# One hybrid decoder layer: p as a unit of the weight stream, six swap tiles, attention pieces at later slots

## The chip, the core and the metric

The kernel runs on one core of a Trainium2 chip. The metric is the device time of one execution in microseconds (us). TensorE (PE) multiplies, VectorE (DVE) and ScalarE (ACT) do elementwise work, GpSimd (POOL) does a little, and SyncE (SP) and ScalarE issue the DMAs.

## The reference

One decoder layer on 512 tokens of width 2048, in float32:

```
h = rms_norm(x); z = h @ w_in      # attn q,k,v (8 heads) and ret q,k,v,gate (8 heads) of 128
a = attention(rotated rms_norm(q), rotated rms_norm(k), v)     # two blocks of 256: causal over all
r = silu(gate) * rms_norm(retention(rotated q, rotated k, v))
x = x + concat(a, r) @ w_o
x = x + (silu(h2 @ w_gate) * (h2 @ w_up)) @ w_down             # h2 = rms_norm(x)
x = x + (p @ w_ple_proj) * sigmoid(rms_norm(x) @ w_ple_gate + b)
```

p is 512 x 256, w_ple_proj 256 x 2048. Each product is made of three products of halves: every float32 operand is split into a high part H (ScalarE copy, written as fp32r) and a low part L = value - H (VectorE), and `mm3` adds HH, HL and LH in PSUM.

## The kernel before, in words

**First stage** (0 to 48 us): `Plain` computes q and k of head pair 0 from xT, whose 16 chunks (`h_chunk`) are loaded, scaled and split into `h` as the weights of the eight units are; step i of `run` calls `beside(i)`, which loads chunks and also forms `first_factors`, the seven combined operands for the next stage. The result goes to DRAM (`zd`).

**Second stage** (to 296 us): groups of seven-product matmuls for v and the gate, written to `vd` and `sgd`.

**Mix stage** (296 to about 795 us): for i = 1 to 7, `projection` computes q and k of head pair i (pairs 0 to 3 attention, 4 to 7 retention) from eight units of weights, each 256 x 512. A unit is four accumulators x two halves x three matmuls; `tick()` opens a slot every two accumulators, so a slot is 12 matmuls and a projection 16 slots. `weights()` keeps up to three units ahead, in the three buffers of `wq`. `heads(i)` puts the pieces of pair i into slots counted from where projection i ended, so they run on TensorE between the matmuls of projection i+1: `turn` transposes q and k (tiles z, line 667) through `tp` (two PSUM banks) into qkH and qkL; `scores` multiplies into `at` (two banks), adds the mask, and makes the softmax rows `pt` (lines 680 to 688); `weights` transposes pt (line 701) into PH and PL; `result` multiplies with v. For the retention pairs the pieces are `load`, `scores`, `normed`, `result`. TensorE keeps program order here; DVE and ACT run in an order that a list scheduler has fixed.

After a projection the four accumulators are evacuated: for attention by `evac` (L627 z, L633 to 637 the norm, L644 to 646 rotation and scaling, with m made by ACT and POOL; z0 is pair 0's input read back from `zd`); for retention by L720 (zr, an ACT copy), two DMAs that swap the halves into mr (L723, L724, issued by ACT), three DVE products and a split into qkH, qkL. z of attention and the tile bc lie in four `rp` buffers; z0, m, zr, mr, praw and pp in the `rm` buffers, four of them. The finished pair is turned into seven factor pairs by `mixed`; they are spilled to DRAM (mix<-o, L188, SP) through the four "o" tiles. `load_ropeT`, at the start of projection 4, transposes rstd (L97) and copies the bank to bc (L586).

**p projection** (759 to 795 us): p is loaded (praw), split (pT), and multiplied with four units w_pp; each accumulator is copied (pp, L858) and stored. Beside it ACT issues 13 DMAs `back` (L801), which load the spilled factors (s<-mix). The pieces of pair 7 run in its slots.

**The rest** (to 2452 us): w_o, SwiGLU, down, gate: seven-product groups, untouched by the change.

Of the kernel before, what the change touches and what calls it, by code (L numbers as in the profile page):

```python
# [11 lines left out]
F32R = mybir.dt.float32r  # L12
# [5 lines left out]
P = 128  # L18
T = 512
D = 2048  # L20
NB = T // P
NC = D // P
NS = D // 512
HD = 128
NPAIR = 4
# [8 lines left out]
def layer_kernel(ctx, tc, x, xT, pT, g_mix, wqk, w_vg, qk_norm, g_ret, w_ow, g_ffn,  # L34
                 w_gu, w_dn, g_ple, w_pl, b_pg, w_pp,
                 ident_c, rope_c, ropeT_c, decay_c, mask_c, out):
    nc = tc.nc
# [444 lines left out]
    def beside(i):  # L482

        if -2 <= i < NC // 2 - 2:
            for k in (2 * i + 4, 2 * i + 5):
                t = h_chunk(k)
                split(h[:, k, 0, :], h[:, k, 1, :], t)
            first.load(i + 2)
        if 2 <= i < 2 + NC // 2:
            first_factors(i - 2)  # L490
        for at, q in ((3, "11"), (6, "12"), (8, "22")):
            if at <= i < at + 4:
                groups[0].load(q, i - at)
        if 7 <= i < 23:
            b, s = divmod(i - 7, NS)
            t = ev_tile("o", 4, name="xn")
            nc.sync.dma_start(t, x[b * P:(b + 1) * P, s * T:(s + 1) * T])
            sq = ev_tile("o", 4, name="sq")
            nc.scalar.activation(sq, t, AF.Square, accum_out=ssq[0][:, b, s:s + 1])
        elif i == 23:  # L500
            rstd_of(ssq[0], rstd[0])
# [29 lines left out]
        return ev2.tile(list(shape), F32, name=name, tag="rp", bufs=4)  # L531

    def rm_tile(name, shape=(P, T), dt=F32):
        return ev2.tile(list(shape), dt, name=name, tag="rm", bufs=4)

    hT = [(h[:, k, 0, :], h[:, k, 1, :]) for k in range(NC)]
    tags = ["l1", "bd", "c"]

    stream = [wqk[i, u] for i in range(1, 2 * NPAIR) for u in range(NC // 2)] + [w_pp[n] for n in range(NS)]
    ready = []  # L540

    def weights():
        while stream and len(ready) < 3:
            tags.append(tags.pop(0))
            raw = rawq.tile([P, 2, T], F32, name="raw", tag=tags[0])
            wh = wq.tile([P, 2, T], F32R, name="wh", tag="wh")
            wl = wq.tile([P, 2, T], F32R, name="wl", tag="wl")
            nc.sync.dma_start(raw, stream.pop(0))
            split(wh, wl, raw)
            ready.append((wh, wl))  # L550
        return ready.pop(0)
# [107 lines left out]
    def attend(z, v, j):  # L659

        got, pts, ps = [], {}, []
# [41 lines left out]
                split(blocks(PH), blocks(PL), tp[:, :nk].rearrange("p (k c) -> p k c", c=P))  # L703

        def result():
            o = weighted(v, ps, j)
            a = ev_tile("A", name="o")
            nc.scalar.activation(a, o, AF.Copy)
            return a
# [27 lines left out]
    def retain(qk, v, j, h):  # L737
# [25 lines left out]
        def normed():  # L763
            hd = slice(j * HD, (j + 1) * HD)
            PH, PL = own["p"]
            r = own["r"] = rp_tile("r", (P, NB, HD))
            ms = stat.tile([P, NB], F32, name="ms")
            for half in range(2):
                o = at_p.tile([P, 2, 2, HD], F32, name="at", tag="at")
                for qb in (2 * half, 2 * half + 1):  # L770
                    for kb in range(qb + 1):
                        at = slice(384 * kb + qb * P, 384 * kb + (qb + 1) * P)
                        matmul(o[:, qb % 2], PH[:, at], v[:, kb, :, hd], start=kb == 0, stop=False)
                        matmul(o[:, qb % 2], PL[:, at], v[:, kb, :, hd], start=False, stop=kb == qb)
                both = slice(2 * half, 2 * half + 2)
                nc.scalar.activation(r[:, both], o[:, :, 0], AF.Copy)
                plus(r[:, both], r[:, both], o[:, :, 1])
            sq = ap.tile([P, T], F32, name="pt", tag="pt", bufs=2)
            for qb in range(NB):
                nc.scalar.activation(sq[:, qb * P:(qb + 1) * P], r[:, qb], AF.Square, accum_out=ms[:, qb:qb + 1])  # L780
            nc.vector.tensor_scalar(ms, ms, 1.0 / HD, EPS, op0=ALU.mult, op1=ALU.add)
            rs = stat.tile([P, NB], F32, name="rs")
            power(rs, ms, NB)
            for qb in range(NB):
                nc.vector.scalar_tensor_tensor(r[:, qb], r[:, qb], rs[:, qb:qb + 1], own["sg"][:, qb],
                                               op0=ALU.mult, op1=ALU.mult)
# [20 lines left out]
        direct = into(s_o, i)  # L807
        factors(*made, lambda p: (direct if p in s_o else spilled)(p))

    def heads(i, made, v):  # L810

        out = []
        if i < NPAIR:
            (turn0, scores0, weights0, result0), (turn1, scores1, weights1, result1) = \
                [attend(made, v, j) for j in range(2)]
            plan = ((7, turn0), (8, lambda: scores0((0, 1))), (10, lambda: weights0((0, 1))),
                    (10, lambda: scores0((2, 3))), (11, turn1), (12, lambda: weights0((2, 3))),
                    (12, lambda: scores1((0, 1))), (14, lambda: out.append(result0())),
                    (14, lambda: weights1((0, 1))), (14, lambda: scores1((2, 3))),
                    (16, lambda: weights1((2, 3))), (18, lambda: out.append(result1())))  # L820
        else:
            (load0, scores0, normed0, result0), (load1, scores1, normed1, result1) = \
                [retain(made, v, j, 2 * (i - NPAIR) + j) for j in range(2)]
            plan = ((1, load0), (5, lambda: scores0((0, 1))), (6, lambda: scores0((2, 3))), (6, load1),
                    (8, normed0), (9, lambda: scores1((0, 1))), (10, lambda: scores1((2, 3))),
                    (11, lambda: out.append(result0())), (12, normed1), (15, lambda: out.append(result1())))
        for n, fn in plan:
            at_slot(n, fn)
        at_slot(plan[-1][0], lambda: mixed(i, out))

    for i in range(2 * NPAIR):
        if i == NPAIR:
            load_ropeT()
        qk = qk_attn(i) if i < NPAIR else qk_ret(i)
        heads(i, qk, v_of(i))
    h_ctx.close()
    pools["s"] = ctx.enter_context(pool("s2"))
    s_o.update({p: factor_tile(p) for p in "1563"})


    pTH = []
    for k in range(2):
        raw = rm_tile("praw")
        nc.sync.dma_start(raw, pT[k * P:(k + 1) * P, :])
        both = ap.tile([P, 2, T], F32R, name="pT", tag="rope" if k == 0 else "pT")
        pTH.append([both[:, 0], both[:, 1]])
        split(*pTH[k], raw)
    for n in range(NS):
        wh, wl = weights()
        accs = [acc_p.tile([P, T], F32, name="acc", tag="acc") for _ in range(NB)]  # L850
        for b in range(NB):
            if b % 2 == 0:
                tick()
            at = slice(b * P, (b + 1) * P)
            for c in range(2):
                mm3(accs[b], pTH[c][0][:, at], pTH[c][1][:, at], wh[:, c, :], wl[:, c, :], c == 0, c == 1)
            t = rm_tile("pp")
            nc.scalar.activation(t, accs[b], AF.Copy)  # L858
            nc.sync.dma_start(ppd[b][:, n], t)
# [145 lines left out]
def _layout(x, p, g_mix, w_in, q_norm, k_norm, g_ret, w_o, g_ffn, w_gate, w_up,  # L1005
# [6 lines left out]
    col = lambda g: c(g.reshape(-1, P).T)  # L1012
    return {
        "x": c(x[0]), "xT": c(x[0].T),
        "pT": c(p[0, 0].T), "g_mix": col(g_mix[0]),
        "wqk": np.concatenate([_units(both(aq, ak)), _units(both(rq, rk))], 0),
        "w_vg": _quarters(np.concatenate([av, rv, rg], 1)),
        "qk_norm": np.stack([q_norm[0], k_norm[0]]), "g_ret": col(g_ret[0]),
# [23 lines left out]
```

## Time and profile before

| | us |
|---|---|
| median of 3 runs | 2452.09 (2449.82 to 2452.33) |
| the profiled execution | 2454.19 |
| its span in the trace | 2452.4 |
| PE / DVE / ACT / POOL busy | 2335.7 / 1957.7 / 1210.5 / 59.8 |

The trace times count from the start of the span; 1.8 us of the execution lie outside it. Busy PE includes matmuls at the lower of its two clock levels.

### The profile page before, as it was taken

The numbers are of one execution on the slowest core, as the hardware profiler recorded it, in microseconds if no ns is written. First come the engines' busy times: TensorE is split into PE (matmuls) and PEld (weight loads), VectorE is DVE, ScalarE is ACT, GpSimd is POOL, SyncE is SP. The second block draws the span as 40 slices with busy tenths as digits, with TensorE's granted clock in tenths as the row PEclk, the third lists the DMA queues.
The fourth block names the chain that finished last, engine by engine and source line by source line (L and its number), as shares of the span: only waits on it lengthen the run. The fifth ranks groups of instructions, "written<-read, shape, count | busy, mean of one in ns | idle before, by whom it ended". The sixth has DMA issues, their size and how long they took to land.

```text
span 2452.4 us, 29384 instructions
## 1 busy us (share of the span) xinstructions
PE 2335.7 (95%) x10470; PEld 1914.4 (78%) x10470; DVE 1957.7 (80%) x2632; ACT 1210.5 (49%) x1887; POOL 59.8 (2%) x63
## 2 busy tenths in 40 slices
PE   8999989988986998999999999999999999999898
PEld 6788868877775887788888888888878878887677
DVE  6888678855554898798888988898878878789897
ACT  7645444434444566455445554555544434346543
POOL 0000022200000000000000000000000000000000
PEclk9999989999997999999999999999999999999999
DMA  8545624446556668444465445644595676777663
GB/s 319 174 143 173 223 85 140 131 126 181 156 158 221 258 201 322 132 145 130 135 189 174 140 127 156 194 155 133 174 395 176 246 282 209 301 240 237 254 208 120
DMA packets 170291, 469.91 MB, mean 192 GB/s; under 512 B 18848, under 2 KB 31520, under 8 KB 165152
## 3 DMA queue, kind: packets, MB, share of 16 engines
q1 hardware_dynamic: 165568, 456.48, 55.4%
q10 hardware_dynamic: 4576, 11.55, 1.5%
q8 instruction: 82, 1.34, 0.2%
q14 instruction: 65, 0.53, 0.1%
HBM read 357.33 MB, written 106.43 MB: 189 GB/s over the span
## 4 chain that ended last, share of the span: by engine, by line
PE 66%; DVE 11%; DMA 7%; issue 2%; ACT 1%; ACTq 0%; SPq 0%; DVEq 0%
PE Y L64 22%; PE Z L64 15%; PE X L64 14%; PE acc L64 11%; DVE wl L55 4%; DVE raw L82 3%; PE at L64 3%; PE tp L69 2%; DMA h<-o 1%; DMA mr<-zr 1%; DMA xin<-x 1%; DVE t L79 1%; ACT wh L54 1%; DMA mix<-o 1%; DVE o L55 1%
## 5 line engine op out<-in xcount | busy, mean ns | idle before, releaser
L54 ACT ACTIVATE wh<-raw 128x1024 fp32r<-128x1024 f32 x726 | 767.4, 1059 | 809.4 <-PE Y L64 280.9
L55 DVE TENSOR_TENSOR wl<-raw,wh 128x1024 fp32r<-128x1024 f32 x726 | 881.7, 1220 | 276.7 <-ACT wh L54 275.0
L64 PE MATMUL Y<-wh,s 128*128 128x512 f32 x2160 | 680.9, 391 | 7.2 <-ACT wh L54 7.2
L64 PEld LDWEIGHTS Y<-wh,s 128*128 128x128 f32 x2160 | 405.3, 188 | 94.0 <-ACT wh L54 11.0
L64 PE MATMUL Z<-wh,s 128*128 128x512 f32 x1504 | 475.0, 391 | 2.3 <-DMA s<-h 2.1
L82 DVE TENSOR_TENSOR raw<-raw 128x1024 f32<-128x1024 f32 x376 | 453.7, 1218 | 28.1 <-DMA raw<-in_w_gu 9.6
L64 PE MATMUL Y<-wl,s 128*128 128x512 f32 x1080 | 425.2, 394 | 3.5 <-DVE wl L55 3.3
L64 PE MATMUL X<-wh,s 128*128 128x512 f32 x1312 | 416.8, 393 | 5.3 <-ACT wh L54 5.3
L64 PEld LDWEIGHTS Z<-wh,s 128*128 128x128 f32 x1504 | 282.3, 188 | 60.7 <-DMA s<-h 2.3
L64 PE MATMUL Z<-wl,s 128*128 128x512 f32 x752 | 297.4, 396 | 6.2 <-DVE wl L55 6.2
L64 PEld LDWEIGHTS X<-wh,s 128*128 128x128 f32 x1312 | 248.1, 189 | 58.4 <-ACT wh L54 7.2
L64 PE MATMUL X<-wl,s 128*128 128x512 f32 x656 | 259.1, 395 | 5.8 <-DVE wl L55 5.7
L64 PEld LDWEIGHTS Y<-wl,s 128*128 128x128 f32 x1080 | 203.2, 188 | 48.4 <-DVE wl L55 7.3
L64 PE MATMUL acc<-h,wh 128*128 128x512 f32 x512 | 166.3, 407 | 11.6 <-ACT zr L720 11.6
L64 PEld LDWEIGHTS Z<-wl,s 128*128 128x128 f32 x752 | 141.7, 188 | 40.7 <-DVE wl L55 12.4
L64 PEld LDWEIGHTS X<-wl,s 128*128 128x128 f32 x656 | 124.1, 189 | 34.4 <-DVE wl L55 8.8
L64 PE MATMUL acc<-wh,h 128*128 128x512 f32 x384 | 124.9, 396 | 0.4 <-DVE e L79 0.4
L64 PEld LDWEIGHTS acc<-h,wh 128*128 128x128 f32 x512 | 98.2, 197 | 33.1 <-ACT zr L720 14.0
L64 PE MATMUL acc<-h,wl 128*128 128x512 f32 x256 | 103.2, 403 | 0.0
L64 PEld LDWEIGHTS acc<-wh,h 128*128 128x128 f32 x384 | 73.2, 191 | 15.8 <-issue 0.8
L54 ACT ACTIVATE o<-t 128x256 fp32r<-128x256 f32 x149 | 56.6, 409 | 45.3 <-DVE t L79 35.6
L64 PE MATMUL acc<-wl,h 128*128 128x512 f32 x192 | 75.7, 394 | 0.0
(188 smaller groups left out, 2121.5 us busy)
## 6 DMA issues: line engine op xcount, KB each, us to landing
raw<-in_w_gu SPq DMA_DIRECT2D x176, 512.0 KB, 4.3
raw<-in_w_dn SPq DMA_DIRECT2D x88, 512.0 KB, 5.9
a<-o SPq DMA_DIRECT2D x154, 256.0 KB, 2.7
raw<-in_wqk SPq DMA_DIRECT2D x64, 512.0 KB, 4.0
s<-a SPq DMA_DIRECT2D x14, 2048.0 KB, 10.7
raw<-in_w_vg SPq DMA_DIRECT2D x48, 512.0 KB, 5.1
raw<-in_w_ow SPq DMA_DIRECT2D x32, 512.0 KB, 5.0
xin<-x SPq DMA_DIRECT2D x64, 256.0 KB, 6.1
```

The costliest lines, as they stand in the source:

```text
L54: nc.scalar.activation(H, src, AF.Copy)
L55: nc.vector.tensor_tensor(L, src, H.bitcast(F32), op=ALU.subtract)
L64: ins = nc.tensor.matmul(*args, **kw)
L69: ins = nc.tensor.transpose(o, a, ident)
L79: nc.vector.tensor_tensor(o, a, b, op=ALU.subtract)
L82: nc.vector.tensor_tensor(o, a, b, op=ALU.add)
```

## The change

p, laid out by the host as one unit like a weight, is one more entry of `stream`, so `weights()` loads and splits it; it keeps one of three buffers from then on, so only two units are kept ahead once four are left. `rm` gets six buffers. The pieces of attention pairs move by one slot, those of pair 0 by three. v is loaded at slot 4 of its pair rather than as the pair begins. `first_factors` runs at steps 4 to 11 rather than 2 to 9.

```diff
--- before.py
+++ after.py
@@ -486,8 +486,8 @@
                 t = h_chunk(k)
                 split(h[:, k, 0, :], h[:, k, 1, :], t)
             first.load(i + 2)
-        if 2 <= i < 2 + NC // 2:
-            first_factors(i - 2)
+        if 4 <= i < 4 + NC // 2:
+            first_factors(i - 4)
         for at, q in ((3, "11"), (6, "12"), (8, "22")):
             if at <= i < at + 4:
                 groups[0].load(q, i - at)
@@ -531,16 +531,16 @@
         return ev2.tile(list(shape), F32, name=name, tag="rp", bufs=4)
 
     def rm_tile(name, shape=(P, T), dt=F32):
-        return ev2.tile(list(shape), dt, name=name, tag="rm", bufs=4)
+        return ev2.tile(list(shape), dt, name=name, tag="rm", bufs=6)
 
     hT = [(h[:, k, 0, :], h[:, k, 1, :]) for k in range(NC)]
     tags = ["l1", "bd", "c"]
 
-    stream = [wqk[i, u] for i in range(1, 2 * NPAIR) for u in range(NC // 2)] + [w_pp[n] for n in range(NS)]
+    stream = [wqk[i, u] for i in range(1, 2 * NPAIR) for u in range(NC // 2)] + [pT] + [w_pp[n] for n in range(NS)]
     ready = []
 
     def weights():
-        while stream and len(ready) < 3:
+        while stream and len(ready) < (3 if len(stream) > NS - 1 else 2):
             tags.append(tags.pop(0))
             raw = rawq.tile([P, 2, T], F32, name="raw", tag=tags[0])
             wh = wq.tile([P, 2, T], F32R, name="wh", tag="wh")
@@ -703,7 +703,7 @@
                 split(blocks(PH), blocks(PL), tp[:, :nk].rearrange("p (k c) -> p k c", c=P))
 
         def result():
-            o = weighted(v, ps, j)
+            o = weighted(v[0], ps, j)
             a = ev_tile("A", name="o")
             nc.scalar.activation(a, o, AF.Copy)
             return a
@@ -770,8 +770,8 @@
                 for qb in (2 * half, 2 * half + 1):
                     for kb in range(qb + 1):
                         at = slice(384 * kb + qb * P, 384 * kb + (qb + 1) * P)
-                        matmul(o[:, qb % 2], PH[:, at], v[:, kb, :, hd], start=kb == 0, stop=False)
-                        matmul(o[:, qb % 2], PL[:, at], v[:, kb, :, hd], start=False, stop=kb == qb)
+                        matmul(o[:, qb % 2], PH[:, at], v[0][:, kb, :, hd], start=kb == 0, stop=False)
+                        matmul(o[:, qb % 2], PL[:, at], v[0][:, kb, :, hd], start=False, stop=kb == qb)
                 both = slice(2 * half, 2 * half + 2)
                 nc.scalar.activation(r[:, both], o[:, :, 0], AF.Copy)
                 plus(r[:, both], r[:, both], o[:, :, 1])
@@ -807,23 +807,26 @@
         direct = into(s_o, i)
         factors(*made, lambda p: (direct if p in s_o else spilled)(p))
 
-    def heads(i, made, v):
-
-        out = []
+    def heads(i, made):
+
+        out, v = [], []
         if i < NPAIR:
             (turn0, scores0, weights0, result0), (turn1, scores1, weights1, result1) = \
                 [attend(made, v, j) for j in range(2)]
-            plan = ((7, turn0), (8, lambda: scores0((0, 1))), (10, lambda: weights0((0, 1))),
-                    (10, lambda: scores0((2, 3))), (11, turn1), (12, lambda: weights0((2, 3))),
-                    (12, lambda: scores1((0, 1))), (14, lambda: out.append(result0())),
-                    (14, lambda: weights1((0, 1))), (14, lambda: scores1((2, 3))),
-                    (16, lambda: weights1((2, 3))), (18, lambda: out.append(result1())))
+            plan = ((8, turn0), (9, lambda: scores0((0, 1))), (11, lambda: weights0((0, 1))),
+                    (11, lambda: scores0((2, 3))), (12, turn1), (13, lambda: weights0((2, 3))),
+                    (13, lambda: scores1((0, 1))), (15, lambda: out.append(result0())),
+                    (15, lambda: weights1((0, 1))), (15, lambda: scores1((2, 3))),
+                    (17, lambda: weights1((2, 3))), (19, lambda: out.append(result1())))
+            if i == 0:
+                plan = tuple((n + 2, fn) for n, fn in plan)
         else:
             (load0, scores0, normed0, result0), (load1, scores1, normed1, result1) = \
                 [retain(made, v, j, 2 * (i - NPAIR) + j) for j in range(2)]
             plan = ((1, load0), (5, lambda: scores0((0, 1))), (6, lambda: scores0((2, 3))), (6, load1),
                     (8, normed0), (9, lambda: scores1((0, 1))), (10, lambda: scores1((2, 3))),
                     (11, lambda: out.append(result0())), (12, normed1), (15, lambda: out.append(result1())))
+        at_slot(4, lambda: v.append(v_of(i)))
         for n, fn in plan:
             at_slot(n, fn)
         at_slot(plan[-1][0], lambda: mixed(i, out))
@@ -832,19 +835,13 @@
         if i == NPAIR:
             load_ropeT()
         qk = qk_attn(i) if i < NPAIR else qk_ret(i)
-        heads(i, qk, v_of(i))
+        heads(i, qk)
     h_ctx.close()
     pools["s"] = ctx.enter_context(pool("s2"))
     s_o.update({p: factor_tile(p) for p in "1563"})
 
 
-    pTH = []
-    for k in range(2):
-        raw = rm_tile("praw")
-        nc.sync.dma_start(raw, pT[k * P:(k + 1) * P, :])
-        both = ap.tile([P, 2, T], F32R, name="pT", tag="rope" if k == 0 else "pT")
-        pTH.append([both[:, 0], both[:, 1]])
-        split(*pTH[k], raw)
+    pTH, pTL = weights()
     for n in range(NS):
         wh, wl = weights()
         accs = [acc_p.tile([P, T], F32, name="acc", tag="acc") for _ in range(NB)]
@@ -853,7 +850,7 @@
                 tick()
             at = slice(b * P, (b + 1) * P)
             for c in range(2):
-                mm3(accs[b], pTH[c][0][:, at], pTH[c][1][:, at], wh[:, c, :], wl[:, c, :], c == 0, c == 1)
+                mm3(accs[b], pTH[:, c, at], pTL[:, c, at], wh[:, c, :], wl[:, c, :], c == 0, c == 1)
             t = rm_tile("pp")
             nc.scalar.activation(t, accs[b], AF.Copy)
             nc.sync.dma_start(ppd[b][:, n], t)
@@ -1012,7 +1009,7 @@
     col = lambda g: c(g.reshape(-1, P).T)
     return {
         "x": c(x[0]), "xT": c(x[0].T),
-        "pT": c(p[0, 0].T), "g_mix": col(g_mix[0]),
+        "pT": c(p[0, 0].T.reshape(2, P, T).transpose(1, 0, 2)), "g_mix": col(g_mix[0]),
         "wqk": np.concatenate([_units(both(aq, ak)), _units(both(rq, rk))], 0),
         "w_vg": _quarters(np.concatenate([av, rv, rg], 1)),
         "qk_norm": np.stack([q_norm[0], k_norm[0]]), "g_ret": col(g_ret[0]),
```

VectorE, in the last half of projection 1 and the evacuation that follows, before: the softmax of pair 0's second head (rows of pt with 384 and 512 columns) and then the four evacuations of pair 1 (z<-acc, the first two are seen).

```order
L688 TENSOR_SCALAR pt<-pt,sm 128x384
L687 RECIPROCAL sm<-sm 128x1
L688 TENSOR_SCALAR pt<-pt,sm 128x512
L627 TENSOR_TENSOR z<-acc,sides 128x512
L55 TENSOR_TENSOR wl<-raw,wh 128x1024
L627 TENSOR_TENSOR z<-acc,sides 128x512
```

The same rows pt in the changed kernel:

```order
L645 TENSOR_TENSOR z<-z,m 128x512
L687 RECIPROCAL sm<-sm 128x1
L637 TENSOR_SCALAR rs<-rs,rstd_83 128x4
L646 TENSOR_TENSOR z<-z,rs 128x512
L683 TENSOR_SCALAR mx<-mx 128x1
L55 TENSOR_TENSOR wl<-raw,wh 128x1024
L688 TENSOR_SCALAR pt<-pt,sm 128x384
L646 TENSOR_TENSOR z<-z,rs 128x512
L687 RECIPROCAL sm<-sm 128x1
L688 TENSOR_SCALAR pt<-pt,sm 128x512
```

They stand behind all four z<-acc and among the last rows (L645, L646) of pair 1's evacuation.

ScalarE at the p projection, before: the last back DMAs (s<-mix), the swaps and splits of pair 7 (mr, qkH), the split of p, then the copies pp of the units n = 0 and 1.

```order
L801 DMA s_6360<-mix_86 128x512
L801 DMA s_6361<-mix_87 128x512
L801 DMA s_6362<-mix_88 128x512
L801 DMA s_6363<-mix_89 128x3584
L54 ACTIVATE qkH<-zr 128x512 x2
L54 ACTIVATE pT<-praw 128x512 x2
L858 ACTIVATE pp<-acc 128x512 x4
L54 ACTIVATE wh<-raw 128x1024
L858 ACTIVATE pp<-acc 128x512 x4
L54 ACTIVATE wh<-raw 128x1024
```

The same stretch of the changed kernel:

```order
L801 DMA s_6356<-mix_87 128x1024
L54 ACTIVATE qkH<-zr 128x512
L855 ACTIVATE pp<-acc 128x512
L801 DMA s_6357<-mix_88 128x1024
L801 DMA s_6355<-mix_86 128x512
L855 ACTIVATE pp<-acc 128x512
L801 DMA s_6356<-mix_87 128x512
L801 DMA s_6357<-mix_88 128x512
L801 DMA s_6358<-mix_89 128x3584
L54 ACTIVATE wh<-raw 128x1024
L54 ACTIVATE qkH<-zr 128x512
L855 ACTIVATE pp<-acc 128x512
```

The split of p is gone from here, and the copies of n = 0 and of the first of n = 1 stand between the back DMAs.

TensorE at the start of projection 4, before: the last matmul of projection 3, the transposes of rstd, then projection 4.

```order
L64 MATMUL acc<-wh,h 128x512
L69 MATMUL tp<-ident,rstd_83 128x128 x4
L64 MATMUL acc<-h,wh 128x512 x2
L64 MATMUL acc<-h,wl 128x512
L64 MATMUL acc<-h,wh 128x512 x2
L64 MATMUL acc<-h,wl 128x512
L64 MATMUL acc<-h,wh 128x512 x2
```

In the changed kernel, the same place:

```order
L64 MATMUL acc<-wh,h 128x512
L69 MATMUL tp<-ident,rstd_83 128x128 x4
L69 MATMUL tp<-ident,pt 128x128 x7
L64 MATMUL acc<-h,wh 128x512 x2
L64 MATMUL acc<-h,wl 128x512
L64 MATMUL acc<-h,wh 128x512 x2
L64 MATMUL acc<-h,wl 128x512
```

The seven transposes of pt (pair 2's second head, rows 2 and 3) now come right behind those of rstd; before, they stood in slot 48, ahead of them.

## Rows read from the trace of the kernel before

**Rows 1.** The page, its part 1: busy us (share) and instructions of each engine.

```profile
PE 2335.7 (95%) x10470; PEld 1914.4 (78%) x10470; DVE 1957.7 (80%) x2632; ACT 1210.5 (49%) x1887; POOL 59.8 (2%) x63
```

**Rows 2.** Waits of TensorE: waiter, releaser, us in total, times, longest us.

```profile
PE acc L64 <- ACT pT L54: 31.5, 1, 31.5
...
PE acc L64 <- ACT zr L720: 11.6, 5, 3.0
PE tp L69 <- DVE z L646: 9.6, 2, 5.3
```

**Rows 3.** Windows: from:to, length; busy us per engine (instructions), clock, DMA share, GB/s.

```profile
312.00:332.00 20.00, 10.27 (x38) 7.88 (x37) 14.52 (x28) 4.50 (x18) 6.76 (x6) 0.66 0.22 66
332.00:496.00 164.00, 162.30 (x805) 136.47 (x803) 128.91 (x301) 77.75 (x231) 35.12 (x36) 1.00 0.40 126
496.00:524.00 28.00, 23.49 (x106) 19.38 (x107) 14.52 (x36) 8.12 (x18) 0.00 (x0) 0.88 0.32 100
540.00:568.00 28.00, 21.68 (x92) 16.98 (x90) 20.36 (x36) 10.80 (x20) 0.00 (x0) 0.94 0.65 190
604.00:620.00 16.00, 10.71 (x40) 8.04 (x39) 11.16 (x18) 5.84 (x10) 0.00 (x0) 0.89 0.68 214
668.00:684.00 16.00, 11.79 (x34) 8.58 (x33) 12.37 (x20) 6.22 (x10) 0.00 (x0) 0.68 0.59 177
```

**Rows 4.** Timeline, TensorE, before and in the p projection: start, us, line, names, [idle <-releaser].

```profile
726.59 0.39 PE L64 MATMUL acc<-h,wl 128*128 128x512 f32 x1
...
727.27 0.39 PE L64 MATMUL acc<-h,wl 128*128 128x512 f32 x1
759.13 0.79 PE L64 MATMUL acc<-wh,pT 128*128 128x512 f32 x1 [31.47 <-ACT pT L54]
...
773.36 0.39 PE L64 MATMUL acc<-wh,pT 128*128 128x512 f32 x1
```

**Rows 5.** Timeline, ScalarE and its DMA issues (ACTq), at the p projection.

```profile
729.76 0.42 ACT L54 ACTIVATE o<-r 128x256 fp32r<-128x256 f32 x1 [3.08 <-DMA mix<-o]
...
743.96 3.52 ACTq L801 DMA_DIRECT2D s<-mix  x4
...
758.45 1.15 ACT L54 ACTIVATE pT<-praw 128x512 fp32r<-128x512 f32 x2 [4.25 <-DMA praw<-in_pT]
```

**Rows 6.** DMA issues of 728 to 760 us: count, KB each, median us to landing.

```profile
s<-mix ACTq DMA_DIRECT2D x9, 512.0 KB, 8.5
```

**Rows 7.** Timeline, TensorE, pair 0's first turn.

```profile
312.94 0.27 PE L69 MATMUL tp<-ident,z 128*128 128x128 f32 x1
```

**Rows 8.** Timeline, VectorE, the last product of pair 0's q and k.

```profile
322.55 1.28 DVE L646 TENSOR_TENSOR z<-z,rs 128x512 f32<-128x512 f32 x2
```

**Rows 9.** Timeline, VectorE, end of pair 0's softmax and pair 1's evacuation.

```profile
354.86 0.55 DVE L682 TENSOR_REDUCE mx<-at 128x1 f32<-128x384 f32 x1
...
357.67 0.49 DVE L688 TENSOR_SCALAR pt<-pt,sm 128x512 f32<-128x512 f32 x1
358.74 0.69 DVE L627 TENSOR_TENSOR z<-acc,sides 128x512 f32<-128x512 f32 x1 [0.58 <-PE acc L64]
...
365.35 0.68 DVE L627 TENSOR_TENSOR z<-acc,sides 128x512 f32<-128x512 f32 x1
...
378.87 0.68 DVE L646 TENSOR_TENSOR z<-z,rs 128x512 f32<-128x512 f32 x1
```

**Rows 10.** Timeline, TensorE, pair 3's second turn.

```profile
516.35 0.66 PE L69 MATMUL tp<-ident,z 128*128 128x128 f32 x4 [2.51 <-DVE qkL L55]
```

**Rows 11.** Timeline, ScalarE, the copy that frees a transposing bank.

```profile
516.78 0.60 ACT L586 ACTIVATE bc<-tp 128x512 f32<-128x512 f32 x1 [1.85 <-PE tp L69]
```

**Rows 12.** Timeline, ScalarE, end of projection 5: a wait on a spill, third copy.

```profile
607.67 0.42 ACT L54 ACTIVATE o<-r 128x256 fp32r<-128x256 f32 x1 [3.52 <-DMA mix<-o]
...
610.19 0.58 ACT L720 ACTIVATE zr<-acc 128x512 f32<-128x512 f32 x1
```

**Rows 13.** Timeline, TensorE, its wait for that third copy.

```profile
610.82 0.73 PE L64 MATMUL acc<-h,wh 128*128 128x512 f32 x2 [2.95 <-ACT zr L720]
```

## The prediction

> **What bounds the kernel now.** I read the engines' busy time first, then TensorE's waits, then the stretches around them. TensorE is busy for 2335.7 of 2452.4 us [rows 1]; VectorE comes second with 1957.7 us. So about 117 us are to be had, and the second question is whose fault they are. In the list of waits three groups belong to the stretch that the change touches [rows 2]: one wait of 31.5 us for the split of p, five of 11.6 us together for the copies zr, and two of 9.6 us for the rotated z. The windows around them show what else goes: idle time is length less busy time, 9.7 us around pair 0's first turn, 4.5 us around pair 3's, then 6.3, 5.3 and 4.2 us at the three changes from one retention projection to the next [rows 3]. The clock column shows a second price: the mean is 0.66, 0.88, 0.94, 0.89 and 0.68 there, against 1.00 between them, so part of each of these windows ran at 1.2 rather than 2.4 GHz. In 312 to 332 us the 38 matmuls took 10.27 us; at the 162.30 us for 805 of the next window they would take 7.7, so the low clock cost about 2.6 us. For the last two windows one minus the clock, times 16 us, bounds it at 1.8 and 5.1 us; I take 1.6 and 4. Lost are then about 12.3 us at pair 0, and about 7.6, 6.9 and 8.2 us at the three changes (the first with 1.3 us for the clock, of at most 1.7). At p, TensorE stops after the matmul of 727.27 us and starts at 759.13 [rows 4].
>
> In the full-speed stretch three matmuls follow in 0.68 us [rows 4], so a slot of 12 is 2.7 us.
>
> **First stage.** `first_factors` two steps later and the same chunks: bytes and elementwise work are the same, only their order differs. The DMA order ahead of the first eight chunks is the same; some ACT and DVE work moves from ahead of a weight split to behind it. I take 0, and 1.5 us either way for one such split.
>
> **Pair 0.** *Gain.* Its first turn moves three slots, 8.2 us, and so from 312.9 to 321.1 us [rows 7]. The last z was ready at 323.8 us (322.55 + 1.28) [rows 8], and with six tiles the m of the last rows no longer waits for the first, which I bound between no help (wait 2.7 us) and enough (0.3). I take 0.8, with no clock loss: of 12.3 us, 11.5 are gained. *Loss.* Its last softmax moves as far, past the end of projection 1. Before, it ended just before the four evacuations of pair 1, which began at 358.74 us [rows 9]; in the changed order its last row stands behind all four z<-acc and nearly all of L645 and L646. From the fourth z<-acc at 365.35 us to the end of the last L646 at 379.55 VectorE spent 14.2 us without a gap; the softmax from 354.86 us to 358.16 adds 3.3 [rows 9]. That makes 17.5 us of VectorE work between the last accumulator and pt. The first accumulator was done at 358.7 us, when VectorE ended a wait of 0.58 us for it, and the last a slot and a half later, with 0.8 us of transposes between: 363.6. Less the 12.3 us, and less 3.7 (my estimate for the scores, transposes and products with v that now come after it), it is done at about 347.6 us. So pt is ready at 365.1 us. TensorE needs it at slot 19: two slots and 3.7 us of pieces after the end of the projection, that is 356.9 us. It waits 8.2 us; I take 7.5, 1.1 us for the row ahead of it, and 2.2 us of low clock as in pair 0 before: a loss of 10.8. The bounds are 2 us (the scheduler's order overlaps waits that I add) and 15 us (the whole 20.8 us of the evacuation [rows 9], less the two slots). **Net +0.7 us, from -4 to +9.**
>
> **Pairs 1 to 3.** One slot later changes little where the softmax is ahead of the evacuation, as in pairs 1 and 3: 0, plus or minus 1 us each. In pair 2 the transposes of pt come right behind those of rstd, which hold one of two `tp` banks until bc is copied. Before, bc was copied only at 516.78 us, because its buffer was still held by a z of pair 3 [rows 11], and the second turn waited 2.51 us in the meantime [rows 10]. With one bank, the transposes for row 3 wait until row 2 has been copied by ACT and subtracted by DVE, which stands behind parts of evac(3). I take 4.7 us, and 2 of low clock: **-6.7 us**, bounds 0 (the subtraction comes early) and -8. Pair 3's waits stay.
>
> **Six swap tiles.** zr takes a swap tile, mr another. With four, the third copy needs the first product done. At the change 4 to 5 the third and fourth copies and their swaps then go ahead of v's loads, since v is loaded four slots later: I take 6.5 of 7.6 us. At 5 to 6 the picture is different [rows 12]: after two copies of zr, ACT waited 3.52 us for a spill of the pair before to leave an "o" tile, did a weight split and qkH, and copied the third at 610.19. The spill stands ahead of it in the changed order too; what the two tiles save is qkH, and at the fourth copy the wait for the swap. TensorE waited 2.95 us for the third [rows 13]. Third copy 1.3 us earlier, fourth 2: 2 to 3.5 us at 5 to 6, 3 to 5 at 6 to 7 (clock with it). Sum **+13 us**; bounds 8 (v's loads do not matter) and 20 (all but 2.7 of the 22.7 us).
>
> **p.** With pT and the first w_pp split long before, the products of n = 0 for the first two accumulators run straight on at 727.7 us. The third needs zr's third copy, behind the spill that ACT waited for until 729.76 us [rows 5], and so about 731.6; the fourth about 735. Then the copies pp stand between the back DMAs in ACT's queue. These were issued until 747.5 us (743.96 + 3.52), and each took 8.5 us to land [rows 5, 6]; an issue waits for a transfer eight places earlier. Between them n = 1 goes accumulator by accumulator. The split of the last unit comes behind the last of them, and then qkH and a copy: 751 to 753 us for n = 2, which before began at 773.36 [rows 4]. That is 20.9 us earlier, and I take 2.4 off for the low clock, as at pair 0, since TensorE works in short pieces: **+18.5 us**, bounds 10 (below) and 24 (n = 2 follows n = 1 without a wait).
>
> The Trainium skill, *DMA: Bandwidth & Descriptors*, section "Issuing engines are not separate DMA queues", says that transfers started by different engines interleave on the same 16 engines, so starting them from several only saves the time of issue. This speaks against a gain as large as the wait: with a busy DMA, ACT's order only decides who waits. By it alone the copies would be paced by the last landing, which gives rival 2. The trace agrees so far as the back transfers took 8.5 us each [rows 6].
>
> **Sum:** 0 + 0.7 - 6.7 + 13 + 18.5 = 25.5 us off the profiled 2454.2: 2428.7. The profiled execution lies 2.1 us above the median of the runs, so **2427 us**. After the p projection the order of instructions is the same, and I cost it at nothing.
>
> **Rivals.** 1. *No new waits:* VectorE reaches pt in pair 0 before TensorE does, and the third bank is free in pair 2. For it: TensorE idles 12 us less earlier and VectorE catches up in these; against it: the order puts four evacuations ahead, and VectorE was busy 128.9 of 164 us over that stretch [rows 3]. Adds 10.8 + 6.7: 2427 - 17 = **2410 us**. The Trainium skill, *TensorE: Matmul & The Clock Gate*, section "Architectural detail: the array is 16× 32×32, not 1× 128×128", says that ACT and DVE take their queues strictly first in, first out; by that VectorE can't bring pt forward, and this rival would need the evacuation itself to be shorter. No row here separates the two.
>
> 2. *The back DMAs hold p:* n = 2 waits for the last of them to land, 747.5 + 8.5 = 756.0, and the landing of the last, larger one for 3 us more (an estimate), then split and copy: 762 us. That is 11.4 us earlier, 9 with the clock, instead of 18.5: **2436 us.** For it: the copies share ACT's queue with the DMAs. Against: only the last accumulators need all copies of n = 1.
>
> 3. *VectorE's backlog in all four attention pairs,* on the other side: evacuations before softmax rows cost pair 0 10.8 us; if pairs 1 to 3 have the same and the two slots do not cover it, the price for each is up to 15 us, 60 in all against 11.5 + 13 + 18.5 = 43 gained: **2469 us**, slower. It decides from 10.8 us a pair. Against it: the order of pair 1 has pt behind two z<-acc only, and pairs 2 and 3 are alike.
>
> **How the numbers follow.** Forecast 0.5 (its own range 2418 to 2435); rival 1 0.2; rival 2 0.2; rival 3 0.05; the rest, a loss that I didn't find, 0.05. A measurement of this kernel can tell about 0.2%, 4.9 us, from no change. Slower than 2457: 0.04; within: 0.05, from rival 3's weaker forms and the rest; faster 0.91. The range reaches over rivals 1 and 2: 2406 to 2442.
>
> **What would show it.** p: no wait for pT; the copies pp between back DMAs; n = 2 at about 752 us in before's time. Swap tiles: TensorE's waits for zr gone at 4 to 5, shorter but there at 5 to 6 and 6 to 7. Pair 0: waits for z under 3 us; a new wait of 7 to 8 us for pt in slot 19, with VectorE unbroken behind it. Pair 2: a new wait for PL at projection 4's start. The prediction is wrong if VectorE's evacuation is over before slot 19, or the back DMAs let n = 2 start only after 760 us.

## The result, and the profile after

The changed kernel takes 2439.63 us (median of 4 runs, 2435.65 to 2440.15) against 2452.21 us before: a ratio of 0.9944, 95% interval 0.9927 to 0.9961. It is faster by 12.6 us where I forecast 25. The profiled execution took 2440.15 us, with a span of 2438.3.

TensorE's busy time and its waits in the changed kernel, as in [rows 1] and [rows 2]:

```profile
PE 2336.2 (96%) x10470; PEld 1911.8 (78%) x10470; DVE 1957.8 (80%) x2631; ACT 1209.1 (50%) x1886; POOL 66.2 (3%) x63
...
PE acc L64 <- ACT pp L855: 15.8, 6, 5.2
...
PE tp L69 <- DVE pt L688: 8.9, 3, 7.2
PE tp L69 <- DVE PL L55: 8.3, 2, 6.0
...
PE acc L64 <- ACT zr L720: 5.4, 6, 1.6
...
PE tp L69 <- DVE z L646: 1.5, 2, 1.1
```

The work is the same (2335.7 us of TensorE before). The 31.5 us for the split of p are gone and 15.8 us for the copies pp stand in their place; zr fell from 11.6 to 5.4 us and z from 9.6 to 1.5; pt is a new group, and PL grew from 0.7 us to 8.3.

Waits alone do not say where time went, because matmuls at the low clock are not in them. So I numbered the matmuls into `acc` in both traces (1440 in each, in the same program order) and compared the times of the same matmul, at places where the same pieces are done in both kernels. The row w_o does the same for a matmul of the group behind p, and the last row is the end of the span:

| place | before | after | difference | this stretch | forecast |
|---|---|---|---|---|---|
| first matmul of projection 1 | 296.52 | 299.25 | +2.7 | +2.7 | 0 |
| projection 2, unit 2, fourth accumulator (pair 0's pieces done) | 380.34 | 384.20 | +3.9 | +1.1 | -0.7 |
| projection 5, unit 0 (pairs 1 to 3 done but for pair 3's last product) | 540.68 | 551.98 | +11.3 | +7.4 | +6.7 |
| projection 7, unit 4 (three changes between retention projections done) | 701.65 | 694.72 | -6.9 | -18.2 | -13 |
| p projection, first matmul of n = 2 | 773.36 | 749.75 | -23.6 | -16.7 | -18.5 |
| p projection, last matmul | 787.41 | 771.53 | -15.9 | +7.7 | 0 |
| group w_o, a wait for wl | 925.48 | 911.70 | -13.8 | +2.1 | 0 |
| end of the span | 2452.4 | 2438.3 | -14.1 | -0.3 | 0 |

The two new waits that the prediction put into pairs 0 and 2, and pair 0's remaining waits for z, in TensorE's timeline of the changed kernel:

```profile
324.54 0.33 PE L69 MATMUL tp<-ident,z 128*128 128x128 f32 x1 [0.31 <-DVE z L646]
326.01 0.77 PE L69 MATMUL tp<-ident,z 128*128 128x128 f32 x5 [1.14 <-DVE z L646]
...
368.60 0.87 PE L69 MATMUL tp<-ident,pt 128*128 128x128 f32 x3 [7.20 <-DVE pt L688]
...
486.46 1.12 PE L69 MATMUL tp<-ident,pt 128*128 128x128 f32 x4 [5.99 <-DVE PL L55]
```

The same pt on VectorE: the fourth accumulator's z, and the two rows of pt that stand behind it.

```profile
351.19 0.68 DVE L627 TENSOR_TENSOR z<-acc,sides 128x512 f32<-128x512 f32 x1
...
368.05 0.41 DVE L688 TENSOR_SCALAR pt<-pt,sm 128x384 f32<-128x384 f32 x1
...
369.16 0.49 DVE L688 TENSOR_SCALAR pt<-pt,sm 128x512 f32<-128x512 f32 x1
```

From the fourth z<-acc to the end of the last pt VectorE works 18.5 us without a gap; the forecast had 17.5.

At p, TensorE's waits and what ScalarE and its DMA issues (ACTq) did meanwhile:

```profile
732.66 0.50 PE L64 MATMUL acc<-wh 128*128 128x512 f32 x1 [4.07 <-ACT pp L855]
...
749.75 0.79 PE L64 MATMUL acc<-wh 128*128 128x512 f32 x1 [5.22 <-ACT pp L855]
...
759.73 0.50 PE L64 MATMUL acc<-wh 128*128 128x512 f32 x1 [1.63 <-ACT pp L855]
...
767.31 0.68 PE L64 MATMUL acc<-wh 128*128 128x512 f32 x1 [2.14 <-ACT pp L855]
```

```profile
744.46 3.12 ACTq L801 DMA_DIRECT2D s<-mix  x3
747.63 1.06 ACT L54 ACTIVATE wh<-raw 128x1024 fp32r<-128x1024 f32 x1 [6.04 <-DMA s<-mix]
...
758.13 1.06 ACT L54 ACTIVATE wh<-raw 128x1024 fp32r<-128x1024 f32 x1 [1.86 <-PE acc L64]
759.10 1.07 ACT L855 ACTIVATE pp<-acc 128x512 f32<-128x512 f32 x2
```

The windows of this stage (columns as in [rows 3]) show why the waits do not add up to the loss:

```profile
728.00:750.00 22.00, 10.00 (x34) 6.95 (x33) 9.56 (x14) 6.74 (x11) 0.00 (x0) 0.85 1.04 363
750.00:760.00 10.00, 8.37 (x31) 6.53 (x32) 4.42 (x9) 4.77 (x10) 0.00 (x0) 0.81 0.93 352
760.00:768.00 8.00, 5.86 (x34) 5.03 (x34) 3.91 (x6) 3.55 (x14) 0.88 (x1) 0.97 0.19 66
768.00:776.00 8.00, 7.25 (x26) 5.56 (x26) 4.49 (x9) 4.63 (x8) 0.13 (x1) 0.82 0.54 164
```

TensorE works 10 of 22 us ahead of n = 2; behind it come two stretches with mean clocks of 0.81 and 0.82. Taken closer, the clock is 0.53 of full speed from 749.75 to 754.10 us, behind the wait of 5.22, and 0.55 from 767.30 to 771.10, behind the wait of 2.14, both near the lower level of 1.2 GHz; between them, with the wait of 1.63, it is 1.00. In the two slow stretches matmuls start 0.43 us apart and not 0.23. Before, n = 2 and n = 3 ran without a gap and with a clock of 1.00: 14.05 us from the first matmul of n = 2 to the last of n = 3. Now it is 21.8. Of the 7.7 us more, 3.8 are the waits of 1.63 and 2.14, and 3.7 are the low clock.

### The profile page after: what moved, and what is told of

Its sections match the earlier page's. It is cut to its first block, busy times and chain, and to the rows that moved or that the text cites. A ratio compares the mean times of both kernels' runs of the same rounds, so it can differ in the third digit from the quotient of the medians.

```text
span 2438.3 us, 29370 instructions
## 1 busy us (share of the span) xinstructions
PE 2336.2 (96%) x10470; PEld 1911.8 (78%) x10470; DVE 1957.8 (80%) x2631; ACT 1209.1 (50%) x1886; POOL 66.2 (3%) x63
## 4 chain that ended last, share of the span: by engine, by line
PE 73%; DVE 11%; DMA 10%; issue 3%; ACT 3%; SPq 0%; ACTq 0%; POOL 0%; DVEq 0%; POOLq 0%
PE Y L64 26%; PE Z L64 17%; PE X L64 16%; PE acc L64 10%; DVE wl L55 4%; PE at L64 2%; DVE raw L82 2%; DMA h<-o 2%; DMA raw<-in_w_dn 2%; PE tp L69 2%; ACT wh L54 1%; DMA raw<-in_w_vg 1%; DMA mix<-o 1%; DVE t L79 1%; DMA s<-mix 1%
## 5 line engine op out<-in xcount | busy, mean ns | idle before, releaser
L64 PEld LDWEIGHTS Y<-wh,s 128*128 128x128 f32 x2160 | 405.5, 188 | 94.0 <-ACT wh L54 11.1
L64 PEld LDWEIGHTS acc<-wh,h 128*128 128x128 f32 x384 | 73.1, 190 | 15.9 <-issue 0.8
L79 DVE TENSOR_TENSOR e<-Y,e 128x512 f32<-128x512 f32 x96 | 62.9, 683 | 13.3 <-PE Y L64 13.3
```

The source lines that it names most:

```text
L64: ins = nc.tensor.matmul(*args, **kw)
L79: nc.vector.tensor_tensor(o, a, b, op=ALU.subtract)
```

## The experiments

Times are medians; ratios are against the kernel before on the same chip, with 95% intervals. "Shift" is the difference of the same `acc` matmul against before, as in the table above.

**1. p as a unit, alone** (`pT_only`). The kernel before with these lines of the change:

```diff
-    ... + [w_pp[n] for n in range(NS)]
+    ... + [pT] + [w_pp[n] for n in range(NS)]
-        while stream and len(ready) < 3:
+        while stream and len(ready) < (3 if len(stream) > NS - 1 else 2):
-    pTH = []
-    for k in range(2):
...
+    pTH, pTL = weights()
```

> The kernel before with one edit only: p as a unit of the weight stream. Theory (the copies pp queue behind the back DMAs and the weight splits on ScalarE, so most of the 31.5 us comes back as smaller waits): 8 to 9 us faster than before, about 2443 us. Rival (the stage alone is worth what I forecast, and something later in the changed kernel took it away): 18 us faster, about 2434 us.

2445.44 us, ratio 0.9972 (0.9959 to 0.9984): 6.6 us less by the medians. TensorE at p and in the first group behind it:

```profile
738.60 0.79 PE L64 MATMUL acc<-wh 128*128 128x512 f32 x1 [6.09 <-ACT zr L720]
...
748.55 0.80 PE L64 MATMUL acc<-wh 128*128 128x512 f32 x1 [7.03 <-ACT pp L852]
...
789.13 0.39 PE L64 MATMUL at<-v,PL 128*128 128x256 f32 x1 [3.21 <-DVE PL L55]
```

The shift goes from -2.3 us ahead of p to -15.0 at its last matmul, so the stage gained 12.7 us, and then to -7.5 at a wait for wl in the group w_o (918.02 against 925.48): 7.5 us are given back behind p, where pair 7's last pieces now wait (3.21 us for PL). n = 2 starts 14.9 us earlier than before, and n = 2 and n = 3 take 13.9 us, nothing more than before: the waits all lie ahead of them here. The theory's size was right; one part of what came back was in a place where I had not looked.

**2. Four swap tiles** (`rm4`). The changed kernel with `tag="rm", bufs=4`.

> The changed kernel with four swap tiles instead of six. Theory (the six tiles are what the three changes between retention projections gained, 17.5 us in the aligned matmuls): 12 to 18 us slower than the changed kernel, with zr waits of 2 to 3 us back. Rival (v's later load freed the ScalarE and DMA queues, the tiles matter little): within 4 us of the changed kernel.

2449.97 us, ratio 0.9993 (0.9982 to 1.0005): by the ratios 12 us of the change's gain go with two tiles. TensorE's waits:

```profile
PE acc L64 <- ACT zr L720: 21.4, 7, 5.6
...
PE acc L64 <- ACT pp L855: 9.3, 2, 7.9
```

zr is back at 21.4 us, and the shift goes only from +12.6 at projection 5 to +9.2 at unit 4 of projection 7, where it fell by 18.2 us in the changed kernel. The theory holds: without the two tiles the three changes give 3.4 us.

**3. first_factors at the old steps** (`factors_early`).

```diff
-        if 4 <= i < 4 + NC // 2:
-            first_factors(i - 4)
+        if 2 <= i < 2 + NC // 2:
+            first_factors(i - 2)
```

> The changed kernel with first_factors back at steps 2 to 9. Theory (the later factors cause the new wait of 2.39 us for s at 87 us and the low clock behind it): that wait is gone and the mix stage starts 2.7 us earlier, about 2437 us. Rival (the 2.7 us come from the run, not from the edit): mix stage starts at 299 us as in the changed kernel, 2439 to 2440 us.

2437.15 us, ratio 0.9945 (0.9924 to 0.9965). The wait in the changed kernel that the theory speaks of, and then the first matmul of projection 1 in this run:

```profile
87.05 0.50 PE L64 MATMUL Z<-wh,s 128*128 128x512 f32 x1 [2.39 <-ACT s L54]
```

```profile
298.20 0.47 PE L64 MATMUL acc<-wh,h 128*128 128x512 f32 x1 [0.39 <-DVE e L79]
```

The wait for s is gone, but projection 1 starts at 298.20 us, not at 296.5. Over all profiles of this study, the eight with the later steps start it at 298.97 to 300.75 us, mean 299.5; the six with the old steps, before among them, at 296.52 to 298.90, mean 297.6. So the later factors cost 1.9 us, and the single pair before and after overstated it by 0.8. In the whole time it is too small to show.

**4. Pair 0 one slot later, not three** (`pair0_plus1`). The two lines `if i == 0: plan = ...` are taken out.

> The changed kernel with pair 0's pieces one slot later like the others, not three. Theory (the softmax of pair 0 falls behind the evacuation of pair 1 only with the three slots): the 7.2 us wait for pt goes, the waits for z come back with about 7 us and the low clock; the whole within 3 us of the changed kernel. Rival (the wait for pt is VectorE's load, not its order, and stays): 6 to 9 us slower than the changed kernel.

2437.16 us, ratio 0.9943 (0.9922 to 0.9965). TensorE's waits at pair 0's first turn:

```profile
323.58 0.33 PE L69 MATMUL tp<-ident,z 128*128 128x128 f32 x1 [3.40 <-DVE z L646]
326.60 0.48 PE L69 MATMUL tp<-ident,z 128*128 128x128 f32 x1 [2.68 <-DVE z L646]
328.07 1.33 PE L69 MATMUL tp<-ident,z 128*128 128x128 f32 x5 [0.99 <-DVE z L646]
```

The waits for z are back with 7.1 us, the wait of 7.20 us for pt is gone with 1.03 us for PL in its place, and from the start of projection 1 to unit 2 of projection 2 the shift falls by 2.3 us, where it grows by 1.1 in the changed kernel. So pair 0's two extra slots moved a wait from z to pt, and in this pair of profiles they cost 3.4 us. The theory holds.

**5. Back DMAs on SyncE** (`backs_SP`).

```diff
-        nc.scalar.dma_start(s_o[p][:, pairs]...
+        nc.sync.dma_start(s_o[p][:, pairs]...
```

> The changed kernel with the 13 back DMAs issued by SyncE instead of ScalarE. Theory (ScalarE's queue holds the copies pp behind the issues of the back DMAs): the waits for pp of 4.07 and 5.22 us go, 4 to 9 us faster than the changed kernel. Rival (the DMA engines' bytes pace the stage, whoever issues): the waits move to SyncE's stores of pp and come back through the swap tiles, within 3 us of the changed kernel.

2438.07 us, ratio 0.9934 (0.9920 to 0.9949). TensorE's waits for pp, and its wait in the group behind p:

```profile
PE acc L64 <- ACT pp L855: 8.3, 3, 5.2
```

```profile
779.03 0.58 PE L64 MATMUL at<-v,PL 128*128 128x256 f32 x1 [3.91 <-DVE PL L55]
```

From unit 4 of projection 7 to the last matmul of p the shift falls by 18.1 us, against 8.9 in the changed kernel: the stage is 9.2 us shorter, and the waits for pp are 8.3 us, not 15.8. The first of them stays (5.18 us at 732.9), the second is 2.89 us (745.5). Behind p pair 7's pieces wait, and at the wait for wl in the group w_o (906.94 us, 911.70 in the changed kernel) 4.8 us of it are left. The shift loses 7 us behind p, and it loses them in one place: TensorE waits 0.69 and 3.91 us for pt and PL, and from 779 to 784 us its mean clock is 0.58. VectorE is what is late there: it works all of the 7 us from 772 to 779, and this PL stands in its order behind weight splits and sums. So the theory's size is shown for the stage, though neither of its two waits is gone. It isn't shown for the whole time: the interval overlaps that of the changed kernel, and the medians lie 1.6 us apart, as the rival has it.

**6. Copies pp by VectorE** (`pp_DVE`).

```diff
-            nc.scalar.activation(t, accs[b], AF.Copy)
+            nc.vector.tensor_copy(t, accs[b])
```

> The changed kernel with the 16 copies pp made by VectorE instead of ScalarE. Theory (the copies wait for their place in ScalarE's queue, behind DMA issues, weight splits and the pieces of pair 7): most of the 15.8 us of waits for pp go, 6 to 12 us faster than the changed kernel. Rival (they wait for the swap tiles, whose stores take 7.1 us to land): the waits stay under VectorE's name, within 3 us of the changed kernel.

2442.23 us, ratio 0.9949 (0.9932 to 0.9966): no gain over the changed kernel. ScalarE and its DMA issues, then VectorE:

```profile
731.90 8.95 ACTq L801 DMA_DIRECT2D s<-mix  x4
740.89 0.63 ACT L54 ACTIVATE qkH<-zr 128x512 fp32r<-128x512 f32 x1 [7.96 <-DMA s<-mix]
```

```profile
741.56 0.69 DVE L55 TENSOR_TENSOR qkL<-zr,qkH 128x512 fp32r<-128x512 f32 x1 [4.86 <-ACT qkH L54]
742.35 0.69 DVE L855 COPY pp<-acc 128x512 f32<-128x512 f32 x1
```

The number is the rival's, the reason is not. Pair 7's qkH stands 7.96 us in ScalarE's queue behind the back DMAs, VectorE waits 4.86 us for it, and the copy stands behind that. Taking the copies off ScalarE doesn't help while something that VectorE needs is still on it.

**7. bc in a swap tile** (`bc_rm`).

```diff
-        bc = rp_tile("bc")
+        bc = rm_tile("bc")
```

> The changed kernel with bc in a swap tile instead of an rp tile. Theory (the bank of rstd's transposes stays taken because bc waits for a z of pair 3, so pair 2's and pair 3's transposes share one bank): the wait of 5.99 us at 486 us and most of the 1.41, 2.31 and 1.41 us after it go, 8 to 11 us faster than the changed kernel. Rival (VectorE's evacuation of pair 3 alone makes PL late): the 5.99 us stay, at most 4 us faster.

2432.96 us, ratio 0.9909 (0.9890 to 0.9928). ScalarE copies bc at once, and TensorE's wait at pair 2 is shorter:

```profile
484.62 0.61 ACT L586 ACTIVATE bc<-tp 128x512 f32<-128x512 f32 x1
```

```profile
485.29 1.12 PE L69 MATMUL tp<-ident,pt 128*128 128x128 f32 x4 [3.49 <-ACT bc L586]
```

The wait is 3.49 us and not 5.99, and pair 3's 1.41, 2.31 and 1.41 us are gone. From the last matmul of projection 3 to the first of projection 5 the shift falls by 2.5 us, where the changed kernel lost 6.7: 9.2 us, and the theory holds, though more than half of pair 2's wait stays, for ACT's squares (m) ahead of bc. In the whole time the medians lie 6.7 us apart, less than the 8 to 11 forecast, and the intervals just touch.

**8. All pieces at their old slots** (`no_shift`). The plan of the changed kernel with every slot one earlier, and without the lines for pair 0.

> The changed kernel with all attention pieces at their old slots, 7 to 18. Theory (the later slots are what put pair 2's transposes behind those of rstd, and pair 0's softmax behind the evacuation): the 5.99 us and the 7.20 us go, pair 0's waits for z come back with 9 us and the low clock; 4 to 7 us faster than the changed kernel. Rival (pair 2's wait comes from the six tiles or v's load): as slow as the changed kernel or slower.

2436.56 us, ratio 0.9933 (0.9918 to 0.9947). Pair 0's waits for z:

```profile
317.28 0.33 PE L69 MATMUL tp<-ident,z 128*128 128x128 f32 x1 [1.28 <-DVE z L646]
321.95 0.47 PE L69 MATMUL tp<-ident,z 128*128 128x128 f32 x1 [4.34 <-DVE z L646]
324.96 0.47 PE L69 MATMUL tp<-ident,z 128*128 128x128 f32 x1 [2.54 <-DVE z L646]
```

The waits for pt and for PL at projection 4 are gone, and pairs 0 to 3 cost the same as before: the shift is +2.9 us at projection 1 and +2.5 at projection 5, where the changed kernel had +11.3. But at the change 4 to 5 (to unit 4 of projection 5) this kernel gains 3.2 us, with a wait of 3.75 us for qkL at 560.69, where the changed kernel gains 9.0 and waits for nothing. That qkL stands on VectorE behind a product that waits 3.32 us (556.94) for the last swap (mr) to land; VectorE has no such wait there in the changed kernel. So the later slots cost 9 us in the attention pairs and give 6 back there, and what is left of the difference at p's end (5.8 us) goes in the group behind it (912.19 against 911.70 us at the same wait). The theory holds for the waits. In the whole time the two are not told apart, and the 4 to 7 us forecast are not shown.

**9. p as a unit and six tiles, nothing else** (`pT_rm6`). Run 1's kernel with `tag="rm", bufs=6`.

> The kernel before with two of the five edits: p as a unit of the weight stream and six swap tiles. Theory (these two make the whole gain, and the later slots, v's slot and the later factors give nothing or take a few us): 2434 to 2437 us against the 2439.6 of the changed kernel. Rival (the third and fourth copies of zr need v's loads out of their way): the wait at the change 4 to 5 stays, 2440 to 2443 us.

2433.68 us, ratio 0.9919 (0.9898 to 0.9940). Two of the five edits give at least what all five give. The shift falls by 11.1 us from projection 5 to unit 4 of projection 7, against 2.9 us in run 1 with four tiles: the tiles alone are worth 8 us there, and with the later slots 15 (18.2 less run 2's 3.4).

**10. v loaded before the slots** (`v_early`). `at_slot(4, lambda: v.append(v_of(i)))` becomes `v.append(v_of(i))`.

> The changed kernel with v loaded before the slots begin, as it was. Theory (the six tiles alone end the wait for zr at the change 4 to 5): within 2 us of the changed kernel. Rival (the swap DMAs must be ahead of v's loads): 3 to 6 us slower, with a wait for zr near 557 us.

2438.38 us, ratio 0.9941 (0.9923 to 0.9959), no wait for zr near 557 us, and a fall of 9.0 us at the change 4 to 5, as in the changed kernel. v's slot does nothing there; the theory holds. At the later two changes the fall is 5.2 us against 9.2, but other runs with six tiles lie between (6.6 in run 7, 7.1 in run 9, 8.6 in run 8), and the whole time does not show it.

**11 and 12. What the runs point to.** Runs 3, 4, 5 and 7 together (`best_plus1`), and runs 3, 5, 7 and 8 together (`best_no_shift`).

> The changed kernel with first_factors at its old steps, pair 0 at one slot like the others, bc in a swap tile and the back DMAs on SyncE. Theory (the four places are apart, and their gains of 2, 2, 7 and 2 to 4 us add): 2425 to 2428 us. Rival (what is gained ahead of the p projection is lost there, since the back DMAs and the w_ow loads pace it): 2431 to 2434 us.

> The same with all attention pieces at their old slots. Theory (with bc out of the way the later slots have nothing left to give, and pair 0 costs the same either way): within 3 us of the run with one slot, 2424 to 2430 us. Rival (one slot later is worth it once the bank is free): 3 to 6 us slower than that run.

2418.78 us, ratio 0.9860 (0.9841 to 0.9879), and 2420.45 us, ratio 0.9868 (0.9850 to 0.9887). Both beat both kernels, and by more than the theory's sum. TensorE's waits in the first:

```profile
PE acc L64 <- ACT pp L853: 8.5, 3, 5.3
PE tp L69 <- DVE z L646: 6.8, 3, 3.3
...
PE acc L64 <- ACT zr L720: 4.4, 6, 1.4
```

Against the changed kernel, run 11 saves 11.1 us in pairs 1 to 3, 9.2 at p, 3.0 in pair 0 and 1.2 in the first stage; it gives back 2.2 at the three changes and 6.3 in the group behind p. The last 4.3 us fall behind the wait in w_o, which no edit touches and where profiles differ by 7 us. One slot or none makes no difference that these runs can tell.

## Why the prediction was half right

The time, 2439.6 us, lies outside the forecast's own range (2418 to 2435) and within the range that reaches over the rivals (2406 to 2442). That is in part luck: without the 5.2 us that the three changes gave beyond their forecast it would be about 2445.

**Right by mechanism, and near in size: pairs 0 to 3.** "Net +0.7 us" for pair 0 came out as a loss of 1.1, within its bounds and made of what it was said to be: z nearly free (1.5 us), a new wait of 7.20 us for pt at 368.6 us (I took 7.5), with VectorE unbroken until then. Pair 2's wait of 4.7 us was 5.99, at projection 4's start and for PL, as said; pairs 1 to 3 together lost 7.4 us against 6.7. Runs 4, 7 and 8 show both causes: with the old slots the waits go, and with the bank freed pair 2's wait shrinks to 3.49 us and pair 3's go. (By the prediction's own figures TensorE needs pt at 356.7 us, not 356.9; nothing hangs on it.)

**Size within its bounds, one reason wrong: the tiles.** "Sum +13 us" was 18.2 in this profile; the other runs with six tiles and the later slots gave 14.1 (run 10) to 18.2 us (run 6). The change 4 to 5 gave 9.0 and not 6.5 us, but not by v's later load, as I had it: with v early it gave 9.0 too (run 10), and with the old slots 3.2 (run 8). Nearly six of it belong to the later attention slots, to which I had given only costs.

**Wrong: p.** "+18.5 us" was 8.9. Its first half held: n = 2 starts 16.7 us earlier (756.7 us, counted in the time of the kernel before, where I had 751 to 753, and under the 760 that I had named as a sign of being wrong). The step that failed is the one that I didn't take: I stopped the count at the first matmul of n = 2 and let n = 2 and n = 3 run as before. Before, TensorE did not wait once in them; now the copies stand behind a split and pair 7's pieces on ScalarE, and TensorE's clock is low behind two of the waits. That gave 7.7 us back. It doesn't come with p as a unit as such: in runs 1 and 2, with four swap tiles, n = 2 starts 14.9 and 2.5 us earlier than before, and n = 2 and n = 3 take 13.9 and 14.1 us. Run 9, with six, starts n = 2 24.7 us earlier and loses 5.0 in them; whether the tiles or the earlier start do it is not told apart. Rival 2 forecast the same size (9 us), by a later start of n = 2 (762 us) that did not come; run 5 shows that it had the culprit nearly right, since without the back DMAs on ScalarE the stage is 9.2 us shorter. The Trainium skill, *DMA: Bandwidth & Descriptors*, section "Issuing engines are not separate DMA queues", says that issuing from several engines saves only the time that the issue takes. The trace agrees so far as the same transfers issued by SyncE left a stage that is 9.2 us shorter (run 5). The time of issue was not small here: in run 6 one row of four issues, with the waits between them, spans 8.95 us on ScalarE, and ScalarE is idle for 7.96 us before qkH.

**Wrong: the first stage.** "I take 0" was a loss of 2.7 us in this pair of profiles, of which the runs show 1.9 to be the edit's: TensorE waits 2.39 us (87.05) for a factor s that is split later. The bound of 1.5 us was too narrow.

**Costed at nothing: what is behind p.** 1.8 us went there. All of it, and 0.3 more, went ahead of the wait for wl in the group w_o (925.48 us before, 911.70 in the changed kernel), 0.75 of it in one more wait for a copy pp at 775.27; from that wait to the end both kernels take 1527 us. Other kernels lose more there: runs 1, 2, 5, 6, 8, 11 and 12 give back 6 to 7 us where the second head of pair 7 is multiplied with v. Run 5 shows how: by waits for pt and PL, and by the low clock behind them.

What stays open: why the order with the old slots meets the last swap before it has landed and the order with the later slots does not; and whether pT's hold on one of three weight buffers delays the copies. At 758.13 us a split waits 1.86 us for TensorE, until the last matmul of n = 2, and two copies stand behind it. Run 5 has the same split and there a wait of 0.27 us, and runs 1 and 2 hold pT in the same way and lose nothing in n = 2 and n = 3, so the hold is not decisive alone; no run gave pT a buffer of its own.

## What to carry to other kernels

When a long wait is taken away, count on to the point where the old and the new order meet again, not to the first instruction that runs early: what filled the wait now competes with what comes after it, and a new wait can cost the lower clock behind it too, as the waits of 5.22 and 2.14 us did here. An engine that computes and also issues DMAs holds its compute for each issue; look for who needs that compute, on other engines too. Delaying a consumer until its input is ready only helps if nothing else moves behind it in another engine's queue: here three slots turned 9.6 us for z into 7.2 us for pt. And a small tile in a pool that is held for long (bc behind pair 3's z) can hold a PSUM bank: one word in the code was worth 9 us in its stretch.

## What the runs showed of the hardware

The start of projection 1 differs between profiles by up to 2.4 us for kernels with the same code ahead of it (296.52 to 298.90 us, six profiles), while the DMA engines' share was 0.84 in the first 20 us and 1.03 in the next. So a difference of 2 us in one pair of profiles is no finding there; eight profiles against six were needed.

An issue of a DMA can stand until an earlier transfer has landed. In the changed kernel three issues of back DMAs by ScalarE start just as an earlier transfer of its queue lands: 739.79 us after 739.77, 744.46 after 744.44, 746.78 after 746.75. What is next in ScalarE's order stands with them: ScalarE is idle for 6.04 us before the weight split at 747.63.
